# Three small edits to a layer kernel: norm sums as two reduced-precision products, a reciprocal moved to a step of its own with a wider gap, and a reordered first product

## The chip, the cores and the metric

The kernel runs on one core of one Trainium2 chip. The number that counts is the device time of one execution in microseconds (us). Three executions of the kernel before took 2320.72, 2321.22 and 2322.16 us; their median is 2321.22 us.

A core has a matrix engine (TensorE, "PE" in the profile; its weight loads are listed apart as "PEld"), an elementwise engine (VectorE, "DVE"), an activation engine (ScalarE, "ACT"), GpSimd ("POOL") and SyncE ("SP"), which here only issues transfers. Each engine runs its own list of instructions in order and waits on semaphores for the others.

## What is computed

One decoder layer on 1024 tokens of 2048 channels, all in float32: a root-mean-square norm (rmsnorm), one combined input projection, two attention groups of eight heads each, their gates, an output projection, a second projection gated by a sigmoid, and a last norm.

```python
hn = rmsnorm(h, norm_mix_g)                       # y * rsqrt(mean(h*h) + eps) * g
proj = hn @ w_in                                  # 2048 -> 16 x 512 columns
# stick-breaking heads: weights exp(log_sigmoid(z) + later sums of log(1 - beta))
# differential heads:
pr = softmax(where(mask, s, -inf))                # two score maps per head
a = pr[:, :, 0] - lam * pr[:, :, 1]
out = rmsnorm(a @ v, subln_g, 1e-5) * 0.8
h = h + concat(sb * silu(g1), out * silu(g2)) @ w_out
gate = sigmoid(rmsnorm(h, norm_ple_g) @ w_ple_gate)
h = h + gate * (p @ w_ple_proj)
return rmsnorm(h, norm_final_g)
```

Every rmsnorm needs, for each token, the sum over channels of the squares. The differential heads need, for each row, the sum of the exponentials, its reciprocal, and for the second map that reciprocal times lam.

## The kernel before

**Layout and precision.** Channels lie on the 128 partitions, tokens along the free dimension, in two halves of 512 tokens (half 1 is worked first). A large product is not done in plain float32: each operand is split into a high part in the matrix engine's reduced format (`F32R`, "fp32r" in the profile) and a low part, the rest. Three products, high x high, high weight x low activation and low weight x high activation, are added up in PSUM. The split itself is one ScalarE copy or cast for the high part and one VectorE subtraction for the low part.

**Stages.** (1) The value and gate columns (`gv`, an object of class `Seven`) are made by a block scheme with seven products instead of eight, called A11, A12, S2, S4, S1, S3 and A22; `product` (L693) issues the twelve matmuls of one of them: for each of four contraction tiles L698 (high x high), L699 (high weight, low x) and L700 (low weight, high x). (2) The query and key columns of each head are made by `unit` (from L280): 32 steps of three matmuls (L294, L295, L296). One head follows the other in `ORDER`, a differential head and a stick-breaking head in turn, first for half 1, then for half 0. (3) The output projection and (4) the gate projection use the block scheme again (`op`, with `gprod` at L1833 and its matmuls L1839 to L1841 in stage 4). (5) The final norm and the output.

**What sets the order.** Around every step of a unit `side.tick()` advances a counter. Work of the attention of earlier heads stands in a list of pairs (tick, function); `side.add` and `side.later` enter functions, and a tick runs what is due. Functions with the same tick keep the order in which they were entered. The order in which this writes instructions of TensorE, VectorE and ScalarE is the order of their queues: it is fixed by hand (`manual_schedule`). The transfers on SP and POOL are placed by a planner. In the block stages `op.step` and `op.soon` do the same in slots of one product.

**The table `TICK`** holds the ticks. Keys that begin with `mid_` hold for the last two heads of half 1 (number 15, differential, and number 7, stick-breaking), whose attention runs while the kernel changes from half 1 to half 0; `end_` is the same for half 0. In that change the activations of half 0 are loaded and split tile by tile: `load_x0` (its split is L1252 on ScalarE and L1253 on VectorE), at ticks from `x0` and `x0_at`.

**A differential head.** For each of four row blocks and two maps: `scores` (matmuls L385 and L386 into z), `top` (L433, mask and row maximum, VectorE), `one` (L441, exponential and row sum l, ScalarE), then for the second map `two`, which issues the reciprocal (L446) and the factor l x lam (L447) on VectorE and the scaling (L448) on ScalarE, and `three` (L453, VectorE). `turn` transposes the weights on TensorE (L488), `parts` splits them (L506 and L507 on ScalarE, L511 and L512 on VectorE), `mix` multiplies them with the values (L530, L533 to L535). `gap` is the number of ticks between a `turn` and the `mix` that uses it.

```python
            def two():
                et, l = es[rb, c]
                V.reciprocal(es[rb, 2], es[rb, 2])
                V.tensor_tensor(l, l, lam, op=ALU.mult)
                A.activation(et[:, vw], et[:, vw], AF.Copy, scale=l[:, 0:1])
```

**Norm sums.** The squares are added up over channel tiles into one tile of 128 partitions x 512 tokens; the sum over partitions, spread to all partitions, is one matmul in plain float32 with a 128 x 128 tile of 1/128 (`ones`, which is the float32 view of `onesr`). There are five of them with 512 columns: two in `norms` (L1208), at tick 17 of the first unit, whose result `rstd_from` (L113 to L117) makes into the root; and one in each of three calls of `norm` (L1851) in stage 4. For those three `load_sums` loads two partial sums (L1870 on SP) and adds them two slots later (L1871, VectorE). `rcol_of` (L1220) makes column copies of the root at ticks 26 and 28.

Of the kernel before, what the change touches and what calls it, by code (L numbers as in the profile page):

```python
# [20 lines left out]
P = 128  # L21
# [16 lines left out]
GVT = 1, 2, 3, 4, 5, 6, 7, 8, 14, 15, 16, 17  # L38
GLAT = {'S4': 4, 'S1': 4, 'S2': 4, 'S3': 3}
TICK = {  # L40
    "neg": 2, "cs": 27, "x0_at": (7, 7, 7, 7), "end_df_soft": (1, 1.5, 4.5, 5.5), "sumlag": 2, "gvx": ((22, 27), (80, 85)),
    "chore": (36, 78, 87), "opx": (8, 12), "turn": 76, "lag": 15, "gap": (4, 6), "parts": (1, 2), "vparts": (3, 4), "sums":
    (0, 2), "squared": (3, 4.5), "norm": (1, 4), "df_scores": (-20, -16, -13, -8, -4, 0, 4, 8), "df_turn": (19, 19), "df_v":
    -1, "df_norm": 44.5, "sb_scores": (-2, 5.5, 13.5, 22), "sb_turn": (32, 36), "sb_v": 23, "df_soft": (1, 1.5, 4, 5.5),
    "sb_stick": (1, 1, 3, 5.5), "taken": (28, 31), "sb_split": (1, 2), "kv": 9, "df_vg": (25, 37, 42, 58, 59.5), "sb_vg":
    (4, 15, 16, 24, 25.5), "q_turn": (-1.0, 5.5, 5, 6.5, 10, 12, 13.5), "k_turn": (-4.5, 8, 8.5, 10, 13.5, 15, 16, 17.5),
# [4 lines left out]
    (18, 21.5, 22, 25, 25.5, 33, 33.5, 38, 42, 46, 50, 54, 58, 62, 66, 70), "begun": (86.5, 91.5, 93.5, 94.5, 93.5),  # L51
    "mid_turn": 76, "mid_lag": 17, "mid_gap": (4, 6), "mid_df_scores": (-20, -16, -9, -8.5, -1, -0.5, 4, 8), "mid_df_turn":
    (19, 17), "mid_df_v": -1, "mid_df_norm": 44.5, "mid_sb_scores": (-3, 5, 12.5, 21), "mid_sb_turn": (32, 36), "mid_sb_v":
    22, "mid_taken": (28, 31), "mid_q_turn": (-1.5, 4.5, 4.5, 5.5, 9.5, 11.5, 12.5), "mid_k_turn": (-1.5, 8, 8.5, 9, 13.5,
    15, 16, 17.5), "end_turn": 76, "end_lag": 15, "end_gap": (4, 6), "end_df_scores": (-23, -16, -15, -8, -4, 0, 4, 8),
    "end_df_turn": (18.5, 19), "end_df_v": -1, "end_df_norm": 44.5, "end_sb_scores": (-2, 6, 13.5, 22), "end_sb_turn": (32,
    36), "end_sb_v": 23, "end_taken": (28, 31), "end_q_turn": (-1.0, 5, 5, 6.5, 10, 12, 13.5), "end_k_turn": (-4.5, 8, 8.5,
    10, 13.5, 15, 16, 17.5),
}
LAM0 = 0.8 - 0.6 * math.exp(0.0)  # L60
NEG = -1.0e30
# [7 lines left out]
def _body(ctx, nc, tc, ap):  # L69
# [275 lines left out]
    def attention(at, pz, half, hd, q, qz, K, KL, VV, sg, vg, rcol):  # L345
# [4 lines left out]
        def tk(nm):  # L350
            return TICK.get(seam + nm, TICK[nm])
# [49 lines left out]
        def weights(rb, c):  # L401
# [34 lines left out]
            def one(mx):  # L436
# [4 lines left out]
                A.activation(et[:, vw], z[:, vw], AF.Exp, bias=mx[:, 0:1], scale=-1.0, accum_out=l[:, c:c + 1])  # L441
                es[rb, c] = et, l[:, c:c + 1]

            def two():
                et, l = es[rb, c]
                V.reciprocal(es[rb, 2], es[rb, 2])  # L446
                V.tensor_tensor(l, l, lam, op=ALU.mult)  # L447
                A.activation(et[:, vw], et[:, vw], AF.Copy, scale=l[:, 0:1])  # L448

            def three():  # L450
# [177 lines left out]
    with tc.tile_pool(name="at", bufs=2) as at, tc.tile_pool(name="pz", bufs=2, space=PSUM) as pz:  # L628
# [23 lines left out]
        class Seven:  # L652
# [37 lines left out]
                else:  # L690
                    low()

            def product(self, u, ph, nm, o, start, tick=False):  # L693
                wh, wl = self.wq.pop((u, ph, nm))
                for k in range(4):
                    xh, xl = self.XC[nm, k]
                    w = slice(k * P, k * P + P)
                    T.matmul(o, wh[:, w], xh, start=start and k == 0, stop=False, skip_group_check=True)  # L698
                    T.matmul(o, wh[:, w], xl, start=False, stop=False, skip_group_check=True)  # L699
                    T.matmul(o, wl[:, w], xh, start=False, stop=k == 3, skip_group_check=True)  # L700
                    if tick:
                        side.tick()

# [243 lines left out]
        for u in range(0, NVG, 2):  # L947
            aa = [pp.tile([P, HALF], F32, name="pa", tag="acc", bufs=2) for _ in range(2)]
            for i in range(2):
                gv.product(u + i, 0, "A11", aa[i], True)  # L950
# [253 lines left out]
        def norms():  # L1204
            t = ev.tile([P, HALF], F32, name="ssq", tag="ssq")
            for hf in (1, 0):
                ps = pp.tile([P, HALF], F32, name="ssps", tag="t")
                T.matmul(ps, ones, ssa[hf], start=True, stop=True)  # L1208
# [637 lines left out]

        def norm(tiles):

            out = tiles[0]
            ps = pp.tile([P, HALF], F32, name="ssps", tag="t")  # L1850
            T.matmul(ps, ones, out, start=True, stop=True)  # L1851

            def roots():
                A.preload_act_table_set("natural_log_exp_and_others")
# [11 lines left out]
        def load_sums(half, tags):  # L1866
            r = []
            for i, (pool, tag, n) in enumerate(tags):
                r.append(pool.tile([P, HALF], F32, name="sums", tag=tag, bufs=n))
                nc.sync.dma_start(r[i], sq_d[half, i])  # L1870
            op.soon.append((op.slot + TICK["sumlag"], lambda: V.tensor_tensor(r[0], r[0], r[1], op=ALU.add)))  # L1871
            return r

        hc = {}
# [536 lines left out]
```

## Time and profile before

| what | value |
|---|---|
| median of three executions | 2321.22 us |
| the profiled execution's own time | 2320.39 us |
| its span, first to last instruction | 2318.3 us |
| TensorE busy | 2303.3 us, 99% of the span |
| VectorE busy | 1795.6 us, 77% |
| ScalarE busy | 1269.6 us, 55% |
| TensorE granted clock, mean | 0.999 |

How to read it: the timeline view lists instructions with start, duration, engine, line, operation, output and inputs, shape, and in brackets the idle time of the engine before it with what ended it ("<-DVE u L1164": a VectorE instruction of that line). Neighbouring instructions of one line are merged into one row with a count. Matmuls are pipelined: a row of 0.39 us does not cost 0.39 us; the next matmul starts 0.23 us later. So what a matmul costs is read from the start of one row to the start of the next, and a stall is a longer step than its neighbours have.

### The profile page before, as it was taken

The numbers are of one execution on the slowest core, as the hardware profiler recorded it, in microseconds if no ns is written. First come the engines' busy times: TensorE is split into PE (matmuls) and PEld (weight loads), VectorE is DVE, ScalarE is ACT, GpSimd is POOL, SyncE is SP. The second block draws the span as 40 slices with busy tenths as digits, with TensorE's granted clock in tenths as the row PEclk, the third lists the DMA queues.
The fourth block names the chain that finished last, engine by engine and source line by source line (L and its number), as shares of the span: only waits on it lengthen the run. The fifth ranks groups of instructions, "written<-read, shape, count | busy, mean of one in ns | idle before, by whom it ended". The sixth has DMA issues, their size and how long they took to land.

```text
span 2318.3 us, 32647 instructions
## 1 busy us (share of the span) xinstructions
PE 2303.3 (99%) x11089; PEld 1928.5 (83%) x11089; DVE 1795.6 (77%) x3118; ACT 1269.6 (55%) x2303; POOL 329.8 (14%) x498
## 2 busy tenths in 40 slices
PE   9999999999999999999999999999999999999998
PEld 7888888888888888887888888888888888888887
DVE  6587776766578888878778878788787988687887
ACT  6423243433356677777776766667733435542555
POOL 2121111111211111101011001110121121111000
PEclk9999999999999999999999999999999999999999
DMA  7687798876888887888676667777899789998975
GB/s 267 212 297 233 253 281 220 215 161 130 208 271 253 244 256 245 254 285 298 199 218 185 184 202 211 202 203 244 260 214 244 249 246 284 321 344 266 306 254 187
DMA packets 258455, 556.66 MB, mean 240 GB/s; under 512 B 28896, under 2 KB 39392, under 8 KB 258288
## 3 DMA queue, kind: packets, MB, share of 16 engines
q1 hardware_dynamic: 180816, 366.55, 49.8%
q0 software_dynamic: 60912, 158.10, 26.0%
q10 hardware_dynamic: 16560, 29.92, 3.5%
q8 instruction: 87, 1.43, 0.2%
q14 instruction: 80, 0.66, 0.1%
HBM read 359.16 MB, written 203.69 MB: 243 GB/s over the span
## 4 chain that ended last, share of the span: by engine, by line
PE 96%; DVE 1%; DMA 1%; ACT 1%; issue 0%; SPq 0%; DVEq 0%; ACTq 0%
PE acc L294 10%; PE acc L296 10%; PE acc L295 10%; PE pbc L698 5%; PE pbc L700 5%; PE pbc L699 4%; PE pa L699 4%; PE pa L700 4%; PE pa L698 4%; PE pc L698 3%; PE pc L700 3%; PE pc L699 3%; PE tp L488 3%; PE pb L1839 2%; PE pb L1840 2%; PE pb L1841 2%
## 5 line engine op out<-in xcount | busy, mean ns | idle before, releaser
L795 ACT CAST wpr<-T 128x512 fp32r<-128x512 f32 x208 | 127.1, 621 | 475.7 <-DVE T L754 394.1
L294 PE MATMUL acc<-xh,whi 128*128 128x512 f32 x768 | 312.9, 407 | 0.0
L296 PE MATMUL acc<-xh,wlo 128*128 128x512 f32 x768 | 301.0, 392 | 0.0
L295 PE MATMUL acc<-xl,whi 128*128 128x512 f32 x768 | 300.7, 392 | 0.0
L296 PEld LDWEIGHTS acc<-xh,wlo 128*128 128x128 f32 x768 | 144.2, 188 | 32.2
L294 PEld LDWEIGHTS acc<-xh,whi 128*128 128x128 f32 x768 | 144.7, 188 | 24.6 <-issue 0.2
L295 PEld LDWEIGHTS acc<-xl,whi 128*128 128x128 f32 x768 | 144.9, 189 | 23.8 <-issue 0.2
L908 POOL DMA_DIRECT2D vg_d<-hc x128 | 89.8, 701 | 445.2 <-DVE hc L1126 263.1
L809 DVE TENSOR_TENSOR wpr<-T,wpr 128x512 fp32r<-128x512 f32 x208 | 142.4, 684 | 6.7 <-ACT wpr L795 3.6
L199 ACT CAST whi<-wraw 128x1024 fp32r<-128x1024 f32 x128 | 134.1, 1048 | 18.1 <-DMA wraw<-w_in 8.5
L795 ACT CAST wpr<-wraw 128x512 fp32r<-128x512 f32 x128 | 78.9, 618 | 107.3 <-DMA wraw<-tw_d 36.7
L441 ACT ACTIVATE et<-z,mx 128x512 f32<-128x512 f32 (+7 forms) x128 | 95.1, 743 | 57.9 <-DVE mx L433 57.7
L433 DVE CUSTOM_DVE_ANT_0 z<-z,wide 128x512 f32<-128x512 f32 (+7 forms) x128 | 97.5, 763 | 32.8 <-PE z L386 29.3
L512 DVE TENSOR_TENSOR awl<-tp,awh 128x256 fp32r<-128x256 f32 (+1 forms) x160 | 92.5, 578 | 32.4 <-ACT awh L507 31.4
L507 ACT CAST awh<-tp 128x256 fp32r<-128x256 f32 (+1 forms) x160 | 80.6, 504 | 43.8 <-PE tp L488 42.8
L809 DVE TENSOR_TENSOR wpr<-wraw,wpr 128x512 fp32r<-128x512 f32 x128 | 86.8, 685 | 17.6 <-ACT wpr L795 17.5
L416 DVE TENSOR_TENSOR_SCAN pt<-pt 128x511 f32<-128x511 f32 (+3 forms) x64 | 86.7, 1354 | 14.4 <-ACT pt L409 13.9
L195 DVE TENSOR_TENSOR wlo<-wraw,whi 128x1024 fp32r<-128x1024 f32 x56 | 68.5, 1223 | 13.9 <-ACT whi L199 13.4
L448 ACT ACTIVATE et<-et,l 128x512 f32<-128x512 f32 (+3 forms) x64 | 49.5, 774 | 42.4 <-DVE l L447 42.4
L535 PE MATMUL av<-awl,v 128*128 128x256 f32 x256 | 72.5, 283 | 0.2 <-DVE awl L512 0.2
L533 PE MATMUL av<-awh,v 128*128 128x256 f32 x256 | 72.1, 282 | 0.1
L534 PE MATMUL av<-awh,v 128*128 128x256 f32 x256 | 72.2, 282 | 0.0
(582 smaller groups left out, 6937.7 us busy)
## 6 DMA issues: line engine op xcount, KB each, us to landing
wraw<-w_in SPq DMA_DIRECT2D x128, 512.0 KB, 4.7
wraw<-w_vg SPq DMA_DIRECT2D x143, 256.0 KB, 3.6
vg_d<-hc POOLq DMA_DIRECT2D x128, 256.0 KB, 5.0
wlo_d<-wlo POOLq DMA_DIRECT2D x56, 512.0 KB, 6.6
wlo<-wlo_d SPq DMA_DIRECT2D x48, 512.0 KB, 3.8
wraw<-w_gate SPq DMA_DIRECT2D x92, 256.0 KB, 5.3
h_d<-hc POOLq DMA_DIRECT2D x56, 256.0 KB, 5.1
wraw<-w_out SPq DMA_DIRECT2D x56, 256.0 KB, 4.7
```

The costliest lines, as they stand in the source:

```text
L199: side.later(1, lambda: A.copy(hi[:, o], raw[:, o]))
L294: T.matmul(acc[c], hi[:, k2, kh, c, :], xh, start=first, stop=False)
L295: T.matmul(acc[c], hi[:, k2, kh, c, :], xl, start=False, stop=False)
L296: T.matmul(acc[c], lo[k2][:, kh, c, :], xh, start=False, stop=last)
L433: V.tensor_tensor_reduce(z[:, vw], z[:, vw], add, -DF_SCALE, 3.0e38, ALU.add, ALU.min, mx)
L441: A.activation(et[:, vw], z[:, vw], AF.Exp, bias=mx[:, 0:1], scale=-1.0, accum_out=l[:, c:c + 1])
L512: V.tensor_tensor(wl[:, o, :], tp[:, o, :], wh[:, o, :].bitcast(F32), op=ALU.subtract)
L698: T.matmul(o, wh[:, w], xh, start=start and k == 0, stop=False, skip_group_check=True)
L699: T.matmul(o, wh[:, w], xl, start=False, stop=False, skip_group_check=True)
L700: T.matmul(o, wl[:, w], xh, start=False, stop=k == 3, skip_group_check=True)
L795: A.copy(t[:, 0], src)
L809: V.tensor_tensor(t[:, 1], src, t[:, 0].bitcast(F32), op=ALU.subtract)
```

## The change

1. **Norm sums.** The five float32 matmuls become ten F32R matmuls: the tile of sums is split into high and low, and `onesr` is multiplied with each. In `norms` the split is a new function `split_sum` at ticks 13 and 14 (a ScalarE copy and a VectorE subtraction for each half, into four tiles of the ring `xt`); `norms` moves from tick 17 to 18 and the two `rcol_of` from 26 and 28 to 27 and 29. In `load_sums` the addition is followed, in the same slot, by a ScalarE copy into the second loaded tile and a VectorE subtraction into a new tile `suml` of the ring `sg`.
2. **The factor l as its own step.** The reciprocal and the factor leave `two` and become `inverse`, due at tick `df_inv` after the second score product: 4, as `two` is, for most heads; 4.5 for the heads at the end, where `two` is at 4.5 also; 2.7 for head 15 of half 1, where `two` is at 4.
3. **Ticks at the change of halves.** `mid_gap` for half 1 goes from 6 to 7 ticks. Of the splits of half 0's activations, the first tile comes two ticks earlier, four of the second quarter one tick later; the third quarter's loads and splits move one tick later (`x0_at` 7 to 8), one of them being net unmoved.
4. **First product.** In the very first product (unit 0, A11) the order of the three terms becomes high x high, low weight x high x, high weight x low x.

```diff
-    "x0_at": (7, 7, 7, 7),
+    "x0_at": (7, 7, 8, 7), "df_inv": 4, "mid_df_inv": 2.7, "end_df_inv": 4.5,
-    "x0": ((5, 5, 13, 12), (5, 6, 13, 14), (5, 6, 15, 16), (5, 5, 13, 11)),
+    "x0": ((3, 5, 13, 12), (6, 7, 14, 15), (5, 6, 14, 16), (5, 5, 13, 11)),
-    "mid_gap": (4, 6),
+    "mid_gap": (4, 7),
...
+            def inverse():
+                l = es[rb, c][1]
+                V.reciprocal(es[rb, 2], es[rb, 2])
+                V.tensor_tensor(l, l, lam, op=ALU.mult)
+
             def two():
                 et, l = es[rb, c]
-                V.reciprocal(es[rb, 2], es[rb, 2])
-                V.tensor_tensor(l, l, lam, op=ALU.mult)
...
+                side.later(tk("df_inv"), inverse)
...
-                    T.matmul(o, wh[:, w], xh, start=start and k == 0, stop=False, skip_group_check=True)
-                    T.matmul(o, wh[:, w], xl, start=False, stop=False, skip_group_check=True)
-                    T.matmul(o, wl[:, w], xh, start=False, stop=k == 3, skip_group_check=True)
+                    terms = [(wh, xh), (wh, xl), (wl, xh)]
+                    if first:
+                        terms[1:] = terms[:0:-1]
+                    for i, (a, x) in enumerate(terms):
+                        T.matmul(o, a[:, w], x, start=start and k + i == 0, stop=k == 3 and i == 2, skip_group_check=True)
...
-                T.matmul(ps, ones, ssa[hf], start=True, stop=True)
+                high, low = halves[hf]
+                T.matmul(ps, onesr, high, start=True, stop=False)
+                T.matmul(ps, onesr, low, start=False, stop=True)
...
-        side.add([(17, norms)])
+        def split_sum(hf):
+            high, low = halves[hf] = [ev.tile([P, HALF], F32R, name=nm, tag="xt", bufs=4) for nm in ("ssah", "ssal")]
+            A.copy(high, ssa[hf])
+            V.tensor_tensor(low, ssa[hf], high.bitcast(F32), op=ALU.subtract)
+
+        side.add([(14 - hf, partial(split_sum, hf)) for hf in (1, 0)] + [(18, norms)])
...
-        side.add([(24, partial(scale_rope, 1, cs)), (26, partial(rcol_of, 1)), (28, partial(rcol_of, 0))])
+        side.add([(24, partial(scale_rope, 1, cs)), (27, partial(rcol_of, 1)), (29, partial(rcol_of, 0))])
...
-            out = tiles[0]
-            T.matmul(ps, ones, out, start=True, stop=True)
+            out, high, low = tiles
+            T.matmul(ps, onesr, high, start=True, stop=False)
+            T.matmul(ps, onesr, low, start=False, stop=True)
...
-            op.soon.append((op.slot + TICK["sumlag"], lambda: V.tensor_tensor(r[0], r[0], r[1], op=ALU.add)))
+            def split():
+                total, high = r
+                V.tensor_tensor(total, total, high.bitcast(F32), op=ALU.add)
+                r.append(at.tile([P, HALF], F32R, name="suml", tag="sg", bufs=3))
+                A.copy(high, total)
+                V.tensor_tensor(r[2], total, high.bitcast(F32), op=ALU.subtract)
+
+            op.soon.append((op.slot + TICK["sumlag"], split))
```

More of the change, by code (lines that the diff above doesn't have):

```diff
@@ L40 @@
 TICK = {
[L41 to L44, printed above, removed]
@@ L54 @@
[L54 to L58, printed above, removed]
+    "neg": 2, "cs": 27, "x0_at": (7, 7, 8, 7), "end_df_soft": (1, 1.5, 4.5, 5.5), "df_inv": 4, "mid_df_inv": 2.7,
@@ new lines @@
+    "end_df_inv": 4.5, "sumlag": 2, "gvx": ((22, 27), (80, 85)), "chore": (36, 78, 87), "opx": (8, 12), "turn": 76, "lag":
+    15, "gap": (4, 6), "parts": (1, 2), "vparts": (3, 4), "sums": (0, 2), "squared": (3, 4.5), "norm": (1, 4), "df_scores":
+    (-20, -16, -13, -8, -4, 0, 4, 8), "df_turn": (19, 19), "df_v": -1, "df_norm": 44.5, "sb_scores": (-2, 5.5, 13.5, 22),
+    "sb_turn": (32, 36), "sb_v": 23, "df_soft": (1, 1.5, 4, 5.5), "sb_stick": (1, 1, 3, 5.5), "taken": (28, 31), "sb_split":
+    (1, 2), "kv": 9, "df_vg": (25, 37, 42, 58, 59.5), "sb_vg": (4, 15, 16, 24, 25.5), "q_turn": (-1.0, 5.5, 5, 6.5, 10, 12,
[5 rows of a table added]
@@ L691, in split, with product @@
                     low()
-            def product(self, u, ph, nm, o, start, tick=False):
+            def product(self, u, ph, nm, o, start, tick=False, first=False):
                 wh, wl = self.wq.pop((u, ph, nm))
@@ L949, in _body @@
             for i in range(2):
-                gv.product(u + i, 0, "A11", aa[i], True)
+                gv.product(u + i, 0, "A11", aa[i], True, first=u + i == 0)
                 s1 = ftile()
@@ L1868, in load_sums @@
             for i, (pool, tag, n) in enumerate(tags):
-                r.append(pool.tile([P, HALF], F32, name="sums", tag=tag, bufs=n))
-                nc.sync.dma_start(r[i], sq_d[half, i])
-            op.soon.append((op.slot + TICK["sumlag"], lambda: V.tensor_tensor(r[0], r[0], r[1], op=ALU.add)))
+                r.append(pool.tile([P, HALF], (F32, F32R)[i], name="sums", tag=tag, bufs=n))
+                nc.sync.dma_start(r[i].bitcast(F32), sq_d[half, i])
+            def split():
[5 more added lines that the diff above has]
+            op.soon.append((op.slot + TICK["sumlag"], split))
             return r
```

13 lines of the change are left out of this document (8 added, 5 removed), and 9 rows, old and new, of the table TICK.

## The prediction

> **What bounds the kernel now.** I read the page first, then the waits of the matrix engine, then the timeline at the places that the change touches.
>
> ```profile
> span 2318.3 us, 32647 instructions
> ...
> PE 2303.3 (99%) x11089; PEld 1928.5 (83%) x11089; DVE 1795.6 (77%) x3118; ACT 1269.6 (55%) x2303; POOL 329.8 (14%) x498
> ...
> PE av L530 <- DVE lead L511: 1.4, 1, 1.4
> PE tp L488 <- DVE et L453: 1.3, 1, 1.3
> ```
>
> TensorE is busy for 99% of the span. A change helps only where it takes steps from TensorE's queue or ends one of its waits. The waits are few: the two longest happen once each, and both lie where the kernel goes from half 1 to half 0. The sum is made against the profiled execution (2320.39 us, its span 2318.3); the median shown is 0.83 above it, and I apply the difference to the median. A measurement of this kernel can tell about 0.2%, 4.64 us, from no change.
>
> **Part one, the norm sums.** What a float32 sum costs is read from its start to the second matmul behind it, less one ordinary step.
>
> ```profile
> 630.23 1.88 PE L1208 MATMUL ssps<-ssa,onesr 128*128 128x512 f32 x4
> ...
> 632.18 0.39 PE L295 MATMUL acc<-xl,whi 128*128 128x512 f32 x1
> ...
> 1975.69 1.02 PE L1851 MATMUL ssps<-sums,onesr 128*128 128x512 f32 x2
> ...
> 1976.78 0.39 PE L1840 MATMUL paz<-cgA11l,wpr 128*128 128x512 f32 x1
> ...
> 2225.30 1.02 PE L1851 MATMUL ssps<-sums,onesr 128*128 128x512 f32 x2
> ...
> 2226.38 0.39 PE L1840 MATMUL pb<-cgS3l,wpr 128*128 128x512 f32 x1
> ...
> 1049.19 0.40 PE L580 MATMUL msq<-sqh,onesr 128*128 128x512 f32 x1
> ...
> 1049.65 0.39 PE L294 MATMUL acc<-xh,whi 128*128 128x512 f32 x1
> ```
>
> The pair in `norms`: 632.18 - 630.23 - 0.23 = 1.72, so 0.86 each. The single ones: 1976.78 - 1975.69 - 0.23 = 0.86 and 2226.38 - 2225.30 - 0.23 = 0.85. The kernel has the replacement already: L580 and the matmul behind it multiply the same `onesr` with a high and a low part, in 1049.65 - 1049.19 = 0.46. So each sum gives 0.40: 0.80 in `norms`, 0.40 at each of these two.
>
> The Trainium skill, in "FP8 and Floating Point Precision", section TensorE Precision Notes, says that true float32 makes four passes through the array. By it a sum would cost 4 x 0.23 = 0.92, and five of them would give 0.3 more than the rows do; the rows (0.86, two records each) are close but decide.
>
> The fifth sum is different.
>
> ```profile
> 2181.95 1.02 PE L1851 MATMUL ssps<-sums,onesr 128*128 128x512 f32 x2
> 2183.03 0.47 PE L1839 MATMUL pc<-cgS4h,wpr 128*128 128x512 f32 x1
> ...
> 2182.20 0.68 DVE L1990 TENSOR_TENSOR hc<-pc,s 128x512 f32<-128x512 f32 x1
> ```
>
> Behind it stands S4 of unit 7, which adds to the same PSUM tile that L1990 reads, until 2182.88. That read starts when the product before the sum is done, so a shorter sum only uncovers it: TensorE would go on at about 2182.93, a gain of 0.10. If something else held 2183.03, the gain is 0.40. I take the middle, 0.25.
>
> The added splits are one ScalarE copy (0.62) and one VectorE subtraction (0.68) for each sum, by the two groups that do the same to weights. They must end before the sum's turn.
>
> ```profile
> L795 ACT CAST wpr<-T 128x512 fp32r<-128x512 f32 x208 | 127.1, 621 | 475.7 <-DVE T L754 394.1
> ...
> L809 DVE TENSOR_TENSOR wpr<-T,wpr 128x512 fp32r<-128x512 f32 x208 | 142.4, 684 | 6.7 <-ACT wpr L795 3.6
> ...
> 1973.02 0.68 DVE L1871 TENSOR_TENSOR sums<-sums 128x512 f32<-128x512 f32 x1
> ...
> 636.91 0.69 DVE L117 SCALAR_TENSOR_TENSOR ssa<-ssq,ssa 128x512 f32<-128x512 f32 x1
> ...
> 638.11 0.95 PE L1220 MATMUL rcps<-onesr,ssa 128*128 128x1 f32 x8
> ```
>
> The tightest is the sum at 1975.69: its addition ends at 1973.70, the copy then at 1974.34, the subtraction at 1975.08, so 0.6 is left. ScalarE stands idle there; behind the copy waits the copy of `paz`, needed only two products later, and behind the subtraction a split of weights that lies several products ahead. At the other two calls the addition stands several products before its sum. In `norms` the splits stand between splits of activations for the last quarter of the unit, and the root's chain, which starts behind a transfer, moves less than 0.1. `rcol_of` comes a tick (0.68) later in order and 0.80 + 0.23 earlier by the matmuls saved: its slack 638.11 - 637.60 = 0.51 falls to between 0.16 and 0.4. I take nothing for all of this; without that cover each late 0.1 costs 0.1. Sum of part one: 0.80 + 0.40 + 0.40 + 0.25 = 1.85, bounds 1.2 and 2.3.
>
> **Part two, the first product.**
>
> ```profile
> 9.31 0.39 PE L698 MATMUL pa<-cA11h,wfh 128*128 128x512 f32 x1
> 9.74 0.50 PE L699 MATMUL pa<-cA11l,wfh 128*128 128x512 f32 x1
> 10.08 0.39 PE L700 MATMUL pa<-cA11h,wfl 128*128 128x512 f32 x1
> 10.31 0.39 PE L698 MATMUL pa<-cA11h,wfh 128*128 128x512 f32 x1
> ...
> 8.93 0.75 DVE L685 SCALAR_TENSOR_TENSOR cA11l<-x,gvec,cA11h 128x512 fp32r<-128x512 f32 x1 [0.25 <-ACT cA11h L679]
> ```
>
> Each of the four low parts of x arrives late; the last is ready at 9.68 and its matmul starts at 9.74. Behind it still stands L700. With L700 ahead of it, in the wait, the next product starts at 10.08 instead of 10.31: 0.23. The other three low parts are bound in the same way and give nothing more, because the next high part is late too. Bounds 0 and 0.3.
>
> **Part three, the change of halves.** Here are the two waits, with VectorE's and ScalarE's queues before them.
>
> ```profile
> 1059.96 0.39 PE L296 MATMUL acc<-xh,wlo 128*128 128x512 f32 x1
> 1061.72 0.51 PE L530 MATMUL av<-lead,v 128*128 128x256 f32 x2 [1.37 <-DVE lead L511]
> ...
> 1055.29 1.41 DVE L1253 SCALAR_TENSOR_TENSOR xl<-xl,gvec,xh 128x512 fp32r<-128x512 f32 x2
> 1056.61 0.69 DVE L433 CUSTOM_DVE_ANT_0 z<-z,wide 128x512 f32<-128x512 f32 x1
> ...
> 1059.15 0.68 DVE L1469 TENSOR_TENSOR qk<-qk,ssa 128x512 f32<-128x512 f32 x1
> 1059.75 0.16 DVE L446 RECIPROCAL l<-l 128x2 f32<-128x2 f32 x1
> ...
> 1061.38 0.29 DVE L511 TENSOR_TENSOR lead<-tp,lead 128x128 fp32r<-128x128 f32 x1 [1.27 <-ACT awh L507]
> ...
> 1060.20 0.72 ACT L448 ACTIVATE et<-et,l 128x512 f32<-128x512 f32 x1 [1.55 <-DVE l L447]
> ...
> 1066.76 0.16 DVE L446 RECIPROCAL l<-l 128x2 f32<-128x2 f32 x1
> ...
> 1069.14 0.61 DVE L453 SCALAR_TENSOR_TENSOR et<-et,l 128x384 f32<-128x384 f32 x1
> ...
> 1069.80 0.33 PE L488 MATMUL tp<-ident,et 128*128 128x128 f32 x1 [1.29 <-DVE et L453]
> ```
>
> Read backwards: TensorE waits for L511; L511 waits 1.27 for ScalarE's L507; ScalarE had waited 1.55, with L507 queued behind L448, for the factor l; and the factor stood in VectorE's queue behind L1253 and L1469. So a two-column reciprocal of 0.16 us holds two engines and then the third.
>
> The new order by the ticks: `inverse` enters the queue two ticks earlier, the tick of the exponential itself. A row block's second maximum (L433) now stands ahead of the pair of L1253 that was at 1055.29, since these splits come a tick later. Laid end to end with the rows' spacing: L433 at 1055.3, a pair of L1253 (1.3), the low part of q (0.65), reciprocal at 1057.85 instead of 1059.75. ScalarE does its exponential, the copy of k and two splits by 1058.5 and then L448; L507 ends at 1059.65. VectorE is by then at the second pair of L1253 and reaches L511 at 1060.0, done by 1060.3. TensorE is due there at 1059.96 + 0.35 = 1060.3. The wait of 1061.72 - 1060.31 = 1.41 goes.
>
> For the second wait, from L511 (1061.38) to the reciprocal is 5.38 before; one L1253 (0.66) now stands behind it, so it comes at 1060.0 + 4.7 = 1064.7. L453 follows 2.38 later before; of that 0.4 was idle waiting for ScalarE, and a second L1253 moves behind: it ends at about 1067.2. TensorE is due at 1066.9: its step of 1.46 in excess shrinks to about 0.3. That is 1.16. Sum 2.57. The same count on the old order puts the two waits at 1.2 and 1.5, so it is good to 0.3; I take 2.6, with bounds 1.1 (one wait only) and 3.2 (both, with the fill steps behind them).
>
> The seventh tick of the gap costs no matmul.
>
> ```profile
> 1073.74 0.68 DVE L473 TENSOR_TENSOR v<-vps,v 128x512 fp32r<-128x512 f32 x1
> ```
>
> It gives the low part of the values (L473, ended at 1074.42) one more tick before `mix` needs it; without it that would be late next, by up to 0.7. What it pushes back is the sum of row blocks 0 and 1 (L549), whose PSUM buffer the turn of blocks 2 and 3 needs: laid end to end that comes 0.1 late. I take nothing; upper bound 0.9. The loads of half 0's activations keep their order, and each had landed before the time at which its split would now run. The `inverse` of all other heads stands where it stood.
>
> **Sum.** 1.85 + 0.23 + 2.6 = 4.7: 2321.22 - 4.7 = 2316.5 us.
>
> **The rivals.**
>
> A. Half the gain at the change of halves. VectorE's queue is nearly full there, so one wait goes and the other moves on to the next block. For it: the second wait hangs on ten VectorE instructions in a row. Against it: the idle 1.27 and 1.55 are waits and not work. Gain 1.85 + 0.23 + 1.2 = 3.3: 2317.9 us.
>
> B. A split comes late for its sum, the one at 1975.69 first.
>
> ```profile
> 1974.82 0.62 ACT L795 CAST wpr<-wraw 128x512 fp32r<-128x512 f32 x1 [3.78 <-DMA hcomb_d<-hc]
> ```
>
> If ScalarE's copy falls behind this cast, which waits for a transfer, it ends at 1976.06 and the subtraction at 1976.8: 1.1 late, 2317.6 us. It decides from 0.6 of delay on. Against it: by the code the copy stands ahead of that cast.
>
> C. The reciprocal blocks VectorE. It now comes soon after the exponential that feeds it; if VectorE gets there first, all behind it waits.
>
> ```profile
> 1057.98 0.19 ACT L441 ACTIVATION_READ_ACCUMULATOR et<-z,mx 128x1 f32 x1
> ```
>
> For the first row block VectorE is done with the maximum at 1057.36 and the sum stands at 1058.17: at most 0.8 of waiting, four blocks 3.2. If all of it reached TensorE and nothing were gained at this place: 2321.2 - 2.1 + 3.2 = 2322.3 us. It turns the sign from 2.1 of added waiting on. Against it: by the count there is other work until 1057.85 for block 0, none waits in blocks 0 and 1. The Trainium skill ("TensorE: Matmul & The Clock Gate", the table at its head) gives VectorE a strict first-in-first-out queue of eight; the wait of L511 above, with the low part of k behind it, agrees.
>
> D. The slower side. The planner places SP's transfers, and the loads of the partial sums already hold up that queue:
>
> ```profile
> SPq L1870 <- DMA sq_d<-rsq: 9.6, 3, 5.4
> ```
>
> Three waits, 9.6 us, with weight loads of the gate stage behind them. In the window before none reached TensorE. If the new tiles move these loads and the waits reach TensorE, the price is up to 9.6: 2316.5 + 9.6 = 2326.1 us. It is slower than before from 4.7 on.
>
> **Chances.** The forecast, with its own range 2315.2 to 2317.3: 0.65, of which 0.53 lie below the bound of 2316.58 and 0.12 above it; the low side also takes in small waits elsewhere that may shift. A 0.16, same. B 0.07, 0.02 faster and 0.05 same. C 0.05, same. D 0.07, slower. So faster 0.55, same 0.38, slower 0.07. The range 2315.0 to 2318.8 takes in the forecast, A and B, and leaves out C and D.
>
> **What would show it.** Right: no L1208 or L1851 record of 0.59, ten records with a step of 0.23; the product after the first one starting at 10.1; L446 about 1.9 earlier against L433, ScalarE's waits for l gone, the two waits of TensorE gone or under 0.4. Wrong: a new wait of TensorE for a subtraction at the sums, for L549 at the turn of blocks 2 and 3, for L1220, or VectorE idle before L446; a later start of weights behind L1870 on SP.

## The result, and the profile after

The changed kernel takes 2316.42 us (median of 15 runs, 2315.5 to 2318.8), the kernel before 2321.14 us in the same measurement (15 runs, 2319.7 to 2322.16). The medians differ by 4.7 us. The ratio is 0.9981, with a 95% interval of 0.9974 to 0.9988, which is between 2.8 and 6.0 us less. The forecast was 2316.5.

The profiled execution of the changed kernel took 2317.11 us, one of the longer ones, that of the kernel before 2320.39, one of the shorter ones. Their spans differ by only 3.0 us. So the total has to be taken from the many runs, and the places from the traces.

The page of the changed kernel, and TensorE's longest waits in its view of the waits (total, number of times, longest):

```profile
span 2315.3 us, 32651 instructions
...
PE 2301.2 (99%) x11089; PEld 1928.1 (83%) x11089; DVE 1799.2 (78%) x3123; ACT 1271.7 (55%) x2308; POOL 329.8 (14%) x498
```

```profile
PE pa L706 <- ACT cA11h L683: 1.6, 2, 1.3
PE warm L919 <- POOL eps L92: 1.0, 1, 1.0
PE ssps L2241 <- DVE sq L2214: 0.7, 1, 0.7
PE av L534 <- DVE awl L516: 0.5, 1, 0.5
PE pc L1854 <- DVE hc L2014: 0.5, 1, 0.5
```

The two waits that led the list before (1.4 and 1.3) are gone from it. Two others are new: 1.3 in the first product, and 0.5 behind the second of the three single norm sums. (Parts one, two and three are those of the prediction: the norm sums, the first product, the change of halves. The texts of the expectations call the change of halves the seam.)

**How the gain is placed.** Both programs issue 11089 matmuls. Set the n-th start of one trace beside the n-th of the other: where the difference steps, time was won or lost. Below, such a change of the difference is called a step, with a minus where time was won. The sums keep their number of records (four, or two each), so the pairing holds around them.

| stretch (time in the kernel before) | step, us | what stands there |
|---|---|---|
| to 10.3 | +0.35 | first product |
| 300 to 320 | -0.34 | a wait of the value stage that before's run had |
| 600 to 645 | -0.54 | the pair of norm sums -0.76, a small wait for low weights +0.22 |
| 1050 to 1130 | -2.06 | the change of halves |
| 1965 to 1980 | -0.41 | first single sum |
| 2170 to 2190 | -0.02 | second single sum |
| 2215 to 2235 | -0.41 | third single sum |
| 2270 to 2290 | +0.29 | a wait in the gate stage that after's run has |
| between these | +0.10 | |

Together -3.04, which is what the spans say. The steps that belong to the change are 0.76 + 2.06 + 0.41 + 0.02 + 0.41 = 3.66 and whatever the first product gives.

The change of halves in the timeline of the changed kernel (start, us, engine, line, operation, in brackets the idle time before it and what ended it):

```profile
1054.14 0.69 DVE L595 TENSOR_TENSOR sg<-sg,avb 128x512 f32<-128x512 f32 x1
1054.75 0.69 DVE L433 CUSTOM_DVE_ANT_0 z<-z,wide 128x512 f32<-128x512 f32 x1
...
1057.28 0.16 DVE L446 RECIPROCAL l<-l 128x2 f32<-128x2 f32 x1
...
1058.09 0.71 ACT L451 ACTIVATE et<-et,l 128x512 f32<-128x512 f32 x1
...
1059.28 0.39 PE L296 MATMUL acc<-xh,wlo 128*128 128x512 f32 x1
1059.48 0.29 DVE L515 TENSOR_TENSOR lead<-tp,lead 128x128 fp32r<-128x128 f32 x1
...
1059.82 0.50 PE L534 MATMUL av<-lead,v 128*128 128x256 f32 x2
...
1064.64 0.62 ACT L451 ACTIVATE et<-et,l 128x384 f32<-128x384 f32 x1 [0.81 <-DVE l L447]
...
1066.06 0.61 DVE L456 SCALAR_TENSOR_TENSOR et<-et,l 128x384 f32<-128x384 f32 x1
...
1066.22 0.83 PE L492 MATMUL tp<-ident,et 128*128 128x128 f32 x3
...
1069.31 0.47 ACT L441 ACTIVATE et<-z,mx 128x256 f32<-128x256 f32 x1 [0.32 <-DVE mx L433]
...
1069.42 0.39 PE L296 MATMUL acc<-xh,wlo 128*128 128x512 f32 x1
1069.93 0.38 PE L379 MATMUL z<-k,q 128*128 128x256 f32 x1
```

The reciprocal now comes 3.14 behind L595 (before: 5.08), with no idle time of VectorE ahead of it. The line of the kernel before is:

```profile
1054.67 0.69 DVE L591 TENSOR_TENSOR sg<-sg,avb 128x512 f32<-128x512 f32 x1
```

ScalarE scales the first row block without waiting, and from L296 to L534 it takes 0.54 in place of 1.76. The second row block still has ScalarE waiting 0.81 for its factor, but the third of the transposes L492 comes only 0.29 later than it would without a wait. New is the last pair: the score product L379 starts 0.51 behind L296 in place of 0.23. It waits for the exponential L441, which ends at 1069.78 and reads the buffer in PSUM (where matmuls leave their results) that L379 writes.

The sums (the second single one, with VectorE's read behind it):

```profile
631.24 0.39 PE L1215 MATMUL ssps<-ssah,onesr 128*128 128x512 f32 x1
631.47 0.39 PE L1216 MATMUL ssps<-ssal,onesr 128*128 128x512 f32 x1
631.71 0.39 PE L1215 MATMUL ssps<-ssah,onesr 128*128 128x512 f32 x1
...
1971.34 0.69 DVE L1893 TENSOR_TENSOR suml<-sums 128x512 fp32r<-128x512 f32 x1 [0.69 <-ACT sums L1892]
...
1973.19 0.40 PE L1866 MATMUL ssps<-sums,onesr 128*128 128x512 f32 x1
...
2179.28 0.39 PE L1867 MATMUL ssps<-suml,onesr 128*128 128x512 f32 x1
...
2179.29 0.68 DVE L2014 TENSOR_TENSOR hc<-pc,s 128x512 f32<-128x512 f32 x1
...
2180.12 0.47 PE L1854 MATMUL pc<-cgS4h,wpr 128*128 128x512 f32 x1 [0.45 <-DVE hc L2014]
```

All ten records are followed by the next one 0.23 later, as long as nothing waits. The subtraction for the first single sum ends at 1972.03, 1.16 ahead of its sum. At 2180 the sum is short and TensorE then stands still for L2014.

### The profile page after: what moved, and what is told of

Read it like the earlier page. It is cut to its first block, busy times and chain, and to the rows that moved or that the text cites. A ratio compares the mean times of both kernels' runs of the same rounds, so it can differ in the third digit from the quotient of the medians.

```text
span 2315.3 us, 32651 instructions
## 1 busy us (share of the span) xinstructions
PE 2301.2 (99%) x11089; PEld 1928.1 (83%) x11089; DVE 1799.2 (78%) x3123; ACT 1271.7 (55%) x2308; POOL 329.8 (14%) x498
## 4 chain that ended last, share of the span: by engine, by line
PE 95%; DVE 2%; DMA 1%; issue 1%; ACT 1%; SPq 0%; DVEq 0%; ACTq 0%
PE pbc L706 14%; PE pa L706 11%; PE acc L294 10%; PE acc L296 10%; PE acc L295 10%; PE pc L706 9%; PE pb L706 4%; PE tp L492 3%; PE av L539 1%; PE z L386 1%; PE z L385 1%; PE av L538 1%; PE av L537 1%; PE pb L1854 1%; PE pb L1855 1%; PE pb L1856 1%
## 5 line engine op out<-in xcount | busy, mean ns | idle before, releaser
L296 PE MATMUL acc<-xh,wlo 128*128 128x512 f32 x768 | 301.1, 392 | 0.0
L296 PEld LDWEIGHTS acc<-xh,wlo 128*128 128x128 f32 x768 | 144.2, 188 | 32.4 <-DVE wlo L195 0.4
L441 ACT ACTIVATE et<-z,mx 128x512 f32<-128x512 f32 (+7 forms) x128 | 95.2, 744 | 59.2 <-DVE mx L433 59.0
L433 DVE CUSTOM_DVE_ANT_0 z<-z,wide 128x512 f32<-128x512 f32 (+7 forms) x128 | 97.7, 765 | 32.7 <-PE z L386 29.3
L706 PE MATMUL pbc<-cA,wpr 128*128 128x512 f32 x480 | 115.7, 390 | 0.2 <-DVE u L1170 0.2
L706 PE MATMUL pc<-cS,wpr 128*128 128x512 f32 x480 | 115.3, 389 | 0.0
L706 PE MATMUL pbc<-cS,wpr 128*128 128x512 f32 x480 | 115.3, 389 | 0.0
L706 PEld LDWEIGHTS pbc<-cA,wpr 128*128 128x128 f32 x480 | 89.9, 188 | 19.8 <-DVE u L1170 1.0
L706 PEld LDWEIGHTS pc<-cS,wpr 128*128 128x128 f32 x480 | 90.1, 188 | 18.7
L706 PEld LDWEIGHTS pbc<-cS,wpr 128*128 128x128 f32 x480 | 90.1, 188 | 18.7
L706 PE MATMUL pbc<-cS2h,wpr 128*128 128x512 f32 x320 | 105.1, 389 | 0.0
L706 PE MATMUL pc<-cS4h,wpr 128*128 128x512 f32 x320 | 105.0, 389 | 0.0
```

The lines of the kernel that those rows point to most:

```text
L296: T.matmul(acc[c], lo[k2][:, kh, c, :], xh, start=False, stop=last)
L433: V.tensor_tensor_reduce(z[:, vw], z[:, vw], add, -DF_SCALE, 3.0e38, ALU.add, ALU.min, mx)
L706: T.matmul(o, a[:, w], x, start=start and k + i == 0, stop=k == 3 and i == 2, skip_group_check=True)
```

## The experiments

**Three theories.** T1, the forecast's: each part gives its gain by itself, the early reciprocal first of all. T2: at the change of halves the later splits of x or the gap do the work, and the reciprocal is beside the point. T3: the gain there hangs on what part one moves ahead of it. Steps of 0.1 to 2 us are below or near what the times can tell, so beside each time stands the step in the trace, read as above against the kernel before.

**1. Part one alone** (the kernel before, with the sums as high and low products).

```
-  T.matmul(ps, ones, ssa[hf], start=True, stop=True)
+  T.matmul(ps, onesr, high, start=True, stop=False)
+  T.matmul(ps, onesr, low, start=False, stop=True)
```

> The kernel before with part one alone: the five norm sums as high and low products. If the replacement is worth what its records say wherever TensorE has work behind it, and nothing where the sum covers a wait: 0.7 to 0.8 us for the pair in the norms, 0.40 at the sum near 1976, 0.0 to 0.1 at the one near 2182 (there a wait for L1990's read of PSUM, about 0.45, shows instead), 0.40 at the one near 2225. Together 1.5 to 1.7: span 2316.6 to 2316.8 beside 2318.3. The change of halves keeps its two waits of 1.37 and 1.29. Rival: all five give 0.40, 2.0 together, and no new wait at 2182. Rival: the splits come late, a wait for the subtraction stands at one of the sums.

Measured: 2319.39 us, ratio 0.9993 (0.9984 to 1.0003). Steps: pair -0.76, then -0.40, 0.00 and -0.41, the change of halves 0.00. At 2182 (timeline of this kernel):

```profile
2182.26 0.39 PE L1861 MATMUL ssps<-suml,onesr 128*128 128x512 f32 x1
...
2182.27 0.68 DVE L2008 TENSOR_TENSOR hc<-pc,s 128x512 f32<-128x512 f32 x1
...
2183.10 0.47 PE L1848 MATMUL pc<-cgS4h,wpr 128*128 128x512 f32 x1 [0.45 <-DVE hc L2008]
```

The sums are worth 1.57 us, in their places, and nothing where one covers a read. (The span is only 0.4 less: this run lost 0.68 in small waits near 612 and 629, and 0.78 at a copy of the gate stage near 1957. Such waits come and go, see below.)

**2. The second single sum in float32 again** (the changed kernel otherwise).

```
-  T.matmul(ps, onesr, high, start=True, stop=False)
-  T.matmul(ps, onesr, low, start=False, stop=True)
+  T.matmul(ps, ones, out, start=True, stop=True)
```

> The changed kernel with the sum near 2180 alone as one float32 product again. If its shortening only uncovers L1990's read: the matmul behind the sum starts at the same time within 0.1, the wait of 0.45 there is gone, the end of the run is the same. Rival: shortening was worth 0.40 there, and the run ends 0.40 later.

Measured: 2317.21 us, ratio 0.9983 (0.9974 to 0.9993). The step at this place is +0.02 against the kernel before and -0.02 in the changed kernel: no difference.

```profile
2178.59 1.02 PE L1867 MATMUL ssps<-sums,onesr 128*128 128x512 f32 x2
...
2178.84 0.68 DVE L2017 TENSOR_TENSOR hc<-pc,s 128x512 f32<-128x512 f32 x1
...
2179.67 0.47 PE L1854 MATMUL pc<-cgS4h,wpr 128*128 128x512 f32 x1
```

In all of them the product starts 0.15 behind the end of the read: 2179.52 and 2179.67 here, 2182.95 and 2183.10 in part one alone, 2179.97 and 2180.12 in the changed kernel, and 2182.88 and 2183.03 in the kernel before. So it was bound by the read already, with no wait to be seen, since the long sum filled the time.

**3. One product moved** to give that read time (the changed kernel, with unit 7's product S1 ahead of unit 6's S4).

```
-            if u < 6:
+            if u < 7:
...
-                p5(7)
```

> The changed kernel with one product of the last gate unit moved: the S1 product of unit 7 stands ahead of the sum near 2180's neighbours, so that L1990's read of PSUM has a product's time more. If the 0.45 of wait behind the shortened sum is only that read: the wait goes, and the run ends up to 0.4 earlier than the changed kernel. Rival: the moved product meets a wait of its own (its weights or its PSUM buffer), and the run ends no earlier.

Measured: 2319.12 us, ratio 0.9993 (0.9983 to 1.0002), worse than the changed kernel. The wait at the sum goes (a step of -0.67 against the changed kernel: 0.45 of wait and the longer steps behind it), and behind the product comes another:

```profile
2184.67 0.62 ACT L801 CAST wpr<-wraw 128x512 fp32r<-128x512 f32 x1 [5.82 <-DMA wraw<-tw_d]
...
2185.32 0.69 DVE L815 TENSOR_TENSOR wpr<-wraw,wpr 128x512 fp32r<-128x512 f32 x1 [4.08 <-ACT wpr L801]
...
2186.66 0.50 PE L1765 MATMUL z<-ph,pwhl 128*128 128x512 f32 x1 [2.71 <-DVE o L1908]
```

L1908 stands in VectorE's queue behind a split of weights that waits 4.08 for ScalarE, and ScalarE had waited 5.82 for the transfer of these weights. The rival holds: 0.67 was given back, and by 2215 the run is 3.7 behind the changed kernel all the same.

**4. Part three alone.**

```
+  side.later(tk("df_inv"), inverse)
...
-  "x0_at": (7, 7, 7, 7)
+  "x0_at": (7, 7, 8, 7), "df_inv": 4, "mid_df_inv": 2.7, "end_df_inv": 4.5
...
-  "x0": ((5, 5, 13, 12), (5, 6, 13, 14), (5, 6, 15, 16), (5, 5, 13, 11))
+  "x0": ((3, 5, 13, 12), (6, 7, 14, 15), (5, 6, 14, 16), (5, 5, 13, 11))
...
-  "mid_gap": (4, 6)
+  "mid_gap": (4, 7)
```

> The kernel before with part three alone: the factor as its own step, the later splits of x for blocks 0 to 2, the gap of seven ticks. If the seam's gain stands by itself: 2.1 us between 1055 and 1085 (1.2 at the first wait, 1.2 at the second, less 0.3 for a new wait of a score product for its PSUM buffer), nothing anywhere else, span about 2316.2. Rival (the forecast): 2.6. Rival: the gain needs part one too, as that alters what the seam starts from: half of it, 1.1.

Measured: 2319.18 us, ratio 0.9992 (0.9983 to 1.0002). The step at the change of halves is -0.80, not -2.1. The second wait went, the first stayed at 1.18 (the last line below). That spoke for T3. Followed back along VectorE's queue, the whole of it runs 1.2 late from 1042 on:

```profile
1041.40 3.50 DVE L1516 TENSOR_TENSOR kl<-qk,k 64x512 fp32r<-64x512 f32 x2
...
1041.60 2.75 POOL L1240 TENSOR_TENSOR cs<-cs,ssa 128x1024 f32<-128x1024 f32 x1 [4.52 <-DMA cs<-rope]
...
1060.99 0.50 PE L534 MATMUL av<-lead,v 128*128 128x256 f32 x2 [1.18 <-DVE lead L515]
```

Taken one by one, the first of the two subtractions lasts 0.68 and the second, from 1042.11, 2.79. Beside it GpSimd scales the angles for the other half; it starts when a transfer lands, and here that was early (4.52 of waiting; 5.72 in the changed kernel). So the run did not tell T1 from T3.

**5. The same kernel again.**

> The kernel with part three alone once more, word for word. In its first profile GpSimd's scaling of the angles (2.75 us from 1041.60) ran beside VectorE's subtraction of k, which took 2.79 us in place of 0.68, and the first wait stayed. If that was the chance landing of one transfer: the scaling starts after 1042.8 this time, the subtraction takes 0.68, the first wait's excess is 0.3 and the seam gives 2.1 by itself. Rival: part three needs part one; the subtraction takes 0.7 and the wait's excess is 1.3 all the same.

Measured: 2318.98 us, ratio 0.9989 (0.9978 to 0.9999).

```profile
1043.07 1.39 DVE L1516 TENSOR_TENSOR kl<-qk,k 64x512 fp32r<-64x512 f32 x2
...
1045.61 2.40 POOL L1240 TENSOR_TENSOR cs<-cs,ssa 128x1024 f32<-128x1024 f32 x1 [6.87 <-DMA cs<-rope]
```

The scaling came after the subtractions, and the step at the change of halves is -2.08. T3 falls: part three gives by itself what it gives in the changed kernel. The chance meeting cost 2.08 - 0.80 = 1.3.

**6. GpSimd kept busy** (the changed kernel, with four products added on a buffer that nobody reads any more).

```
+  for _ in range(4):
+      G.tensor_tensor(sw, sw, sw, op=ALU.mult)
```

> The changed kernel with four GpSimd products of 128x512 added, on a buffer that nobody reads any more: two about 1037, the others behind the scaling of the angles. They change no result. If VectorE and GpSimd exclude each other where both work in SBUF: the subtractions of q and of the squares near 1037 to 1039 (0.69 each before) last until the product beside them ends, up to 1.9 each; VectorE's reads of PSUM and its operations with one SBUF input keep their times. Rival: each engine keeps its times (1.2 and 0.69), and the long subtraction of the earlier run had another cause.

Measured: one run of 2317.9 us.

```profile
1036.30 1.76 DVE L1523 TENSOR_TENSOR q<-qk,q 64x512 fp32r<-64x512 f32 x1
...
1036.45 2.52 POOL L1542 TENSOR_TENSOR sw<-sw 128x512 f32<-128x512 f32 x2
...
1038.09 1.42 DVE L575 TENSOR_TENSOR sql<-sqv,sqh 128x512 fp32r<-128x512 f32 x1
```

The two subtractions, 0.69 each without this, take 1.76 and 1.42. The pair on GpSimd ends at 1038.97 and the second subtraction at 1039.51, 0.54 behind it: it did its work once GpSimd was done. GpSimd's second product, begun while the first subtraction was still at work, took 1.38, the first one 1.06. TensorE then waited 0.97 in front of the matmul at 1041.01 and 0.80 at the first wait of the change of halves, and that gave 1.46 in place of 2.06. Behind the scaling of the angles a split of x at 1046.21 took 1.19 in place of 0.75 beside the third product, and the scan behind it 2.09 in place of 0.42, across two transfers that GpSimd issues and the fourth product; which of these held the scan is not shown. That VectorE's subtractions and GpSimd's products hold each other up is shown by these rows, in one execution.

**7 to 9. One element of part three taken back at a time** (the changed kernel otherwise).

```
-  "mid_df_inv": 2.7          +  "mid_df_inv": 4
```

> The changed kernel with the factor's step put back to the tick after the old one (4 instead of 2.7 ticks into each head of the change of halves), the rest as changed. If the early reciprocal is what removes the two waits: 1.85 us of the seam's gain are lost (waits for the scaled exponentials of 1.2 and 0.4 us and one of 0.9 for a PSUM buffer, by the queues laid end to end), the span about 2317.2. Rival: the later splits of x do the main part, and the loss is under 0.6.

```
-  "mid_gap": (4, 7)          +  "mid_gap": (4, 6)
```

> The changed kernel with a gap of six ticks as before. If the seventh tick gives the low part of the values its time: TensorE waits some 0.7 us for L477's v at the mix of a later row block, and the seam ends 0.5 later (span about 2315.8). Rival: the tick only moves work, and the seam ends within 0.15 of the changed kernel. Rival: the seventh tick costs, and the seam ends 0.1 or more earlier.

```
-  "x0_at": (7, 7, 8, 7), "x0": ((3, 5, 13, 12), (6, 7, 14, 15), (5, 6, 14, 16), (5, 5, 13, 11))
+  "x0_at": (7, 7, 7, 7), "x0": ((5, 5, 13, 12), (5, 6, 13, 14), (5, 6, 15, 16), (5, 5, 13, 11))
```

> The changed kernel with the splits of x for half 0 at their ticks of before. If a row block's maximum ahead of the splits is part of the gain: VectorE comes later to the factor, waits of about 0.6 at the mix and 1.0 at a turn come back, and the seam ends 0.9 later (span about 2316.2). Rival: the early reciprocal alone does it, and the seam ends within 0.15 of the changed kernel.

| taken back | median, us | ratio (95%) | step at the change of halves | lost of 2.06 | counted |
|---|---|---|---|---|---|
| factor early | 2319.02 | 0.9991 (0.9981 to 1.0000) | -0.34 | 1.72 | 1.85 |
| seventh tick | 2317.62 | 0.9986 (0.9977 to 0.9996) | -1.38 | 0.68 | 0.5 |
| later splits | 2317.38 | 0.9984 (0.9975 to 0.9993) | -1.34 | 0.72 | 0.9 |

The waits that come back, one kernel to a fence in this order:

```profile
1060.47 0.51 PE L534 MATMUL av<-lead,v 128*128 128x256 f32 x2 [1.52 <-DVE lead L515]
...
1071.23 0.39 PE L379 MATMUL z<-k,q 128*128 128x256 f32 x1 [0.78 <-ACT et L441]
```

```profile
1071.81 0.38 PE L534 MATMUL av<-lead,v 128*128 128x256 f32 x1 [0.71 <-DVE v L477]
```

```profile
1059.52 0.51 PE L533 MATMUL av<-lead,v 128*128 128x256 f32 x2 [0.75 <-DVE lead L514]
...
1067.10 0.33 PE L491 MATMUL tp<-ident,et 128*128 128x128 f32 x1 [0.79 <-DVE et L455]
```

T1 holds for the factor, the largest element. T2 holds in part: without the later splits or the seventh tick a third of the gain goes. The losses add up to 3.12, more than 2.06: they hide behind each other. The queues laid end to end gave each loss within 0.2; the single waits less well (for the late factor 1.2, 0.4 and 0.9 were counted; 1.52, 0.29 and 0.78 came).

**10. Four splits moved once more,** chosen by that count.

```
-  (6, 7, 14, 15), (5, 6, 14, 16), (5, 5, 13, 11)
+  (6, 9, 14, 14), (3, 6, 14, 16), (5, 6, 13, 11)
```

> The changed kernel with four splits of x for half 0 at other ticks, found by laying the queues of the seam end to end: the second of block 1 two ticks later and its fourth one earlier, the first of block 2 two ticks earlier, the second of block 3 one later. By the count the waits of the seam (0.31, 0.29, 0.28, and the short one for v) all go, and the seam ends 0.78 earlier. Rival: the waits move on to other tiles, and the seam ends within 0.2 of the changed kernel. The time itself can show neither: 0.78 is 0.03%.

Measured: 2318.35 us, ratio 0.9987 (0.9978 to 0.9997). The step at the change of halves is -0.13: nearly all of the gain is gone.

```profile
1052.73 0.75 DVE L1268 SCALAR_TENSOR_TENSOR xl<-xl,gvec,xh 128x512 fp32r<-128x512 f32 x1 [1.94 <-ACT xh L1267]
...
1057.80 0.45 PE L385 MATMUL z<-k,q 128*128 128x384 f32 x1 [1.21 <-ACT et L441]
```

The split moved two ticks earlier now stands ahead of the squares of the norm, and VectorE waits 1.94 there for ScalarE's half of it. The exponential behind is late, and a score product waits 1.21 for its buffer. The waits did not just move on to other tiles: neither the expectation nor its rival had this.

**11. Part two alone** (the order of the terms, in the first product).

```
-  (wh, xh), (wh, xl), (wl, xh)
+  (wh, xh), (wl, xh), (wh, xl)
```

> The kernel before with part two alone. The forecast: from the start of the last low-x matmul of the first product to the first matmul of the second product 0.34 instead of 0.57, so 0.23 less; the start of the whole product moves with the landing of its first transfers by some tenths, whatever the order. If the low weights land late, the new order makes TensorE wait for them at the second matmul and the gain is gone: the second matmul then starts later than 9.3 and the second product not before 10.3. Nothing else in the run moves by more than 0.1.

Measured: 2320.32 us, ratio 1.0001 (0.9991 to 1.001). The second matmul starts at 5.46 and the second product at 9.83, so the low weights are not late. But here the last low x was on time too (steps of 0.23 all through the last block), so the 0.34 in place of 0.57 cannot be seen in this run. In the changed kernel it can:

```profile
8.83 0.50 PE L706 MATMUL pa<-cA11h,wfh 128*128 128x512 f32 x1 [1.34 <-ACT cA11h L683]
9.17 0.40 PE L706 MATMUL pa<-cA11h,wfl 128*128 128x512 f32 x1
9.62 0.50 PE L706 MATMUL pa<-cA11l,wfh 128*128 128x512 f32 x1
9.96 0.39 PE L706 MATMUL pa<-cA11h,wfh 128*128 128x512 f32 x1
...
10.66 0.39 PE L706 MATMUL pa<-cA11h,wfh 128*128 128x512 f32 x1
```

From the late low x of the third block (9.62) to the next block 0.34: there the order does what was said. When the product as a whole is done hangs on the transfers. Over all profiles the second product starts at 9.94 to 10.47 in the old order (four runs, mean 10.22) and at 9.66 to 10.66 in the new (nine runs, mean 10.06). The means differ by 0.16, the runs of one order by up to 1.0: the gain is not measured. One more place moved in this run, where nothing was changed: the change of halves lost 0.29, 0.20 of it in front of a score product.

## Why the prediction was right, and where it was not

- **The total.** 2316.5 against 2316.42, in the forecast's own range. The traces bear out 3.66 of the 4.7 us, and for the first product (0.23 predicted) nothing that can be told from its scatter. Whether the remaining 1.0 is real stays open: the interval of the difference, 2.8 to 6.0, holds both. The kernel of experiment 2, which in the traces gains the same within 0.1, came out 3.8 below the kernel before. So the hit within 0.1 is in part luck: the terms were too high by about 1.0, and the measured median lay as much below what the traces account for. By the prediction's own measure of 0.2%, the result lies on the bound between faster and same: the ratio 0.9981 is just short of it, the difference of the medians, 4.72, just beyond 4.64. That there is a gain at all is clear of noise.
- **The pair in the norms and two of the single sums.** 0.80, 0.40 and 0.40 predicted; 0.76 to 0.80, 0.40 to 0.41 and 0.40 to 0.41 measured in the nine profiles that have them. Right, and so is the cover of the splits: no wait for a subtraction stands at any sum, and the spare at the sum named as the tightest was 1.16, not 0.6, in this run. But it varies: in the eight other profiles with the split it is between 0.06 (experiment 3) and 1.16. And in the changed kernel another one was tighter: the second subtraction of the pair in `norms` ends at 631.31, 0.40 ahead of its sum at 631.71.
- **The sum at 2181.95.** This step failed. I saw that its shortening uncovers L1990's read, let TensorE go on 0.05 behind the read's end, and took the middle of 0.10 and 0.40. It goes on 0.15 behind that end in four kernels, and the kernel before was on that line already (2182.88 and 2183.03). The gain is 0.0; the lower end should have been zero, and the mechanism named should have decided, not a middle.
- **The first wait of the change of halves.** 1.41 predicted, 1.22 measured, from the step of 1.76 to 0.54. The count of VectorE's queue was right: L511 done by 1060.3, measured 1059.77 + 0.57 (what the run had gained by 1050) = 1060.34. The size failed on TensorE's side: I let the step shrink to 0.35, as if TensorE came to this product just when L511 was done. L296 itself came another 0.11 earlier (the step of 0.34 in front of 1059.04 is 0.23 in the changed kernel), and the product starts 0.05 behind the end of the subtraction. So about 0.2 of wait was left. Counted with that 0.11, the product starts 1.33 earlier.
- **The second wait.** 1.16 predicted with a rest of 0.3; 1.17 measured with a rest of 0.29.
- **What is late next.** I named the values' low part and the sum of row blocks 0 and 1. The turn of blocks 2 and 3 has no wait, and the values cost about 0.1. The one that came is the score product L379 behind the exponential L441: 0.25 to 0.28, and 0.11 in the longer step behind it, in all runs with the whole of part three. The second wait had covered it. In the changed kernel these are 0.39, most of the missing 0.5: 2.6 predicted, 2.06 measured; about 0.1 more is the first wait.
- **The seventh tick** was set at nothing, with the values late by up to 0.7 without it: 0.71 of wait, and 0.68 lost, when it is taken back.
- **Rival A** (half the gain): the kernel keeps 2.06 of 2.6, so no; but taking back either the later splits or the tick gives just this. **Rival B:** no late split. **Rival C:** no idle time of VectorE stands ahead of the reciprocal at 1057.28. **Rival D:** in the waits of SP's queue the loads of the partial sums stand as before, and no wait of TensorE goes back to them:

```profile
SPq L1886 <- DMA sq_d<-rsq: 9.6, 3, 5.4
```

- **What would show it.** The signs for the sums came. "L446 about 1.9 earlier against L433" was badly put, as L433 moves too; against L595 it is 1.94 earlier. "The product after the first one at 10.1" came at 10.66, by a landing. ScalarE's wait for the factor is gone in the first row block only.

## What to carry to other kernels

Where work that is to be shortened stands ahead of something that waits for another engine, look in the trace whether what follows already starts at a constant distance behind that engine's end: then the shortening gives nothing, though no wait is to be seen. When a stall goes, ask for every buffer that is released in the shadow of it, not only for the operands. And where an edit is worth less than a run's scatter, pair the instructions of two traces one by one, and repeat the run before believing that two edits need each other.

## What the runs showed of the hardware that I had not expected

VectorE and GpSimd stopped each other. A subtraction of 0.68 took 2.79 us beside a GpSimd product, which itself took 2.75 in place of 2.40 (experiment 4); with GpSimd kept busy, 1.76 and 1.42 in place of 0.69. All three were done 0.54 to 0.56 behind the end of GpSimd's product. Beside the scaling at 1045.61 in experiment 5 VectorE's three instructions each had an input in PSUM, and kept their times (0.69, 0.28 and 0.30). The Trainium skill, "SBUF — State Buffer", section "Who interferes with whom", says that a VectorE instruction with two inputs in SBUF and a GpSimd instruction that reads SBUF take a shared pair of ports in turn, each for the whole instruction, and that whichever starts first blocks the other. These rows agree that one engine waits for the whole of the other's instruction. They do not agree on which one: in experiment 6 the first subtraction is recorded as starting 0.15 ahead of GpSimd's product, and still it was the one that waited. In the kernel before and in the changed one the scaling missed the subtractions; in the changed one it started at 1042.91, when the last of them, from 1042.21, was just done (0.69). It starts when the angles have landed, 4.52 to 7.12 us behind their issue over all thirteen profiles. In one of them the subtraction paid for it (experiment 4). In experiment 6 the scaling began 0.25 ahead of the end of the last subtraction, which kept its 0.69; the scaling took 2.52.

Beside that, three places come and go from run to run: the end of the first product (9.66 to 10.66), single waits of 0.3 to 0.6 us in the value stage (near 310, 463 or 612), and a copy of the gate stage near 1957 that TensorE waits for, which cost between 0 and 1.39 us in the twelve profiles set beside the first. The three large ones there (0.78, 0.99 and 1.39) were all in kernels with part one, though six others with it lost at most 0.16 and the three without it at most 0.21; whether part one makes that wait more likely was not tried. These waits are as large as the scatter between the runs of one kernel, and some of them may well be its cause; that was not tried either.
